# An expert block on one core: where the held scatter of a light quad runs, and the order of the output stage

## The chip, the cores and the metric

One core of a Trainium2 chip runs the whole program. The metric is the device time of one execution in microseconds. The kernel before takes 493.15 us, the median of three runs.

## The reference, cut to what matters

```python
D_MODEL, SEQ, N_GROUPS, EXPERTS_PER_GROUP, TOP_K_INNER, D_EXPERT = 1024, 512, 4, 8, 2, 256

def hierarchical_moe(t, w_group, b_group, w_inner, b_inner, w_gate, w_up, w_down):
    group_p = softmax(t @ w_group + b_group)
    g_w, g_idx = lax.top_k(group_p, 1)
    inner_all = einsum('nd,gde->nge', t, w_inner) + b_inner
    inner_p = softmax(inner_all of the chosen group)
    e_w, e_idx = lax.top_k(inner_p, TOP_K_INNER)
    e_w = e_w / sum(e_w)
    combine = g_w * one_hot(g_idx) * (e_w at e_idx)
    y = zeros_like(t)
    for g in range(N_GROUPS):
        hg = silu(einsum('nd,edf->nef', t, w_gate[g])) * einsum('nd,edf->nef', t, w_up[g])
        y = y + einsum('nef,efd->nd', hg * combine[:, g, :, None], w_down[g])
    return y

def reference(x, ...):
    h = rmsnorm(x, mix_norm)
    x = x + concat([forgetting_attention(h ...), rg_lru(h ...) * gelu(...)]) @ w_out
    x = x + hierarchical_moe(rmsnorm(x, ffn_norm), ...)
    return rmsnorm(x, final_norm)
```

There are 512 tokens in four tiles of 128 and 32 experts. Each expert has three matrices of 1024 x 256 (gate, up) and 256 x 1024 (down) in float32, 3 MB together.

## The kernel before, in words

The attention, the recurrent group, the output projection and the router take about the first half of the span. The change lies in the second half, the experts.

**Quads.** The 32 experts are worked on in eight quads of four. An expert takes at most 32 tokens of each half of the sequence (CAP = 32); a quad's four experts stand side by side on the four groups of 32 partitions. Quads 0 to 5 (groups 0 to 2) are heavy: each treats the two halves of the tokens (hf 0 and 1) one after the other. Quads 6 and 7 (group 3) are light: the experts with few tokens have been sorted there, and one pass of 32 places serves both halves. Quad 6 is the `if light:` branch of the loop over `quads[:-1]`, quad 7 the code behind the loop.

**One pass** consists of these steps:
- `gate_up` multiplies the gathered tokens `xg` with gate and up weights, k = 0 to 7, into one PSUM tile `pg` (tag "mm").
- `places` makes two things out of the 0/1 matrices `s16`: the *front* matmuls against `ident16` transpose them into a PSUM tile `pt` (tag "lg"), and ScalarE copies that to `sT` (the matrix with which results are scattered back to tokens); the *weight* matmuls against `c16` fetch each place's combine weight into `pc`. DVE's `cj`, `cs` and `cw` reduce `pc` to one number for each place. For one half (`len(hfs) == 1`, heavy) `pc` is columns 256 on of the same tile `pt`; for both halves at once (light) `pc` is a tile of its own (tag "tr", printed as ps_pv).
- `hidden` makes `hg`: a tanh on ScalarE, and two operations on DVE, the second of which needs `cw`. `hidden_T` transposes it on TensorE, DVE copies it to `hgT`.
- `down` multiplies with the down weights and splits the result into a high and a low part `y` (ScalarE, then DVE). `scatter` multiplies `sT` with both parts into two PSUM tiles and DVE adds them to `xs`, the running sum (one token tile and one half `n` of the 1024 columns for each add).

**Held scatter.** The last scatters of a quad aren't run at its end. They go into `held` and are run by the next quad, behind its gate-up step k = 0: `held.pop()()`. For a heavy quad these are the scatters of y10 and y11 (second half), for quad 6 those of y1 (both halves).

**Order.** TensorE's instructions and the weight loads keep their program order in this part (`pinned[0] = 1`). DVE's and ScalarE's are ordered by the scheduler of the framework, which tracks what each tile is written and read by and sets the waits. From quad 7's `hidden` on (`pinned[0] = 2`) DVE and ScalarE keep the program order too.

**Loads.** Gate, up and down weights come in 512 KB transfers on SP's queue, in program order, into 18 buffers of 1 MB (`slot` 12, `slot_m` 4, `slot_b` 2); `load_next` issues the next quad's sixteen gate-up loads and eight down loads. A load waits for its buffer's last reader and for room in the queue.

**Output stage.** Behind quad 7's down products: `scatter_to` fills pa and pc (token tiles 0 and 1, columns 0 to 511 and 512 to 1023), pb and pd (token tiles 2 and 3). For pd the running sum has been put into PSUM ahead, by two products with the identity (`mm(pd[t], ident, xs[:, 2 + t, h1], True, False)`), which stand between `hidden_T` and the down products. `square_out` sums squares on ScalarE (and multiplies columns 0 to 511 by `gfin` on POOL), `rsqrt_parts` makes the reciprocal root of a half's sums (ScalarE's square root, small operations on DVE), `write_out` scales (DVE for columns 512 on, with `gfin`; ScalarE for the others) and issues the output's transfer.

Of the kernel before, what the change touches and what calls it, by code (L numbers as in the profile page):

```python
# [53 lines left out]
def block_kernel(ctx, tc, x, mix_norm, w_in, b_forget, conv_w, conv_b, w_a, b_a, w_x, b_x, lru_lambda,  # L54
# [13 lines left out]
    def mm(out_, lhsT, rhs, start, stop):  # L68
        pin(nc.tensor.matmul(out=out_, lhsT=lhsT, rhs=rhs, start=start, stop=stop))  # L69
# [23 lines left out]
    def act(out_, in_, func, **kw):  # L93
        pin(nc.scalar.activation(out=out_, in_=in_, func=func, **kw), 2)  # L94
# [729 lines left out]
    def pst(tag):  # L824
        return psum({"gu": "mm", "gz": "lg", "y": "tr", "tr": "pv"}[tag])
# [159 lines left out]
    def gate_up(pg, xt, gu, q, ks):  # L985
        for k in ks:
            for e in range(4):
                mm(pg[e * CAP:(e + 1) * CAP, :], xt[:, k, q * 4 + e, :],
                   gu[k][e], k == 0, k == KT - 1)

    def places(g, q, hfs, s16):

        n = NS * 3 if g else 12
        pt = pst("gz")
        pc = pst("tr")[:, 0:n] if len(hfs) > 1 else pt[:, 2 * P:2 * P + n]
        sq = [(2 * h + t, s16[h][:, t, q * 4:q * 4 + 4, :].rearrange("p e c -> p (e c)")) for h in hfs for t in range(2)]
        rows = [slice(e * CAP, (e + 1) * CAP) for e in range(4)]
        for i, (t, v) in enumerate(sq):
            for r in rows:
                mm(pt[r, i * P:(i + 1) * P], v[:, r], ident16, True, True)  # L1000
        for i, (t, v) in enumerate(sq):
            c = c16[:, t, 1:].rearrange("p g i e -> p (g i e)") if g else c16[:, t, 0, :, q * 4:q * 4 + 4]
            for r in rows:
                mm(pc[r], v[:, r], c, i == 0, i == len(sq) - 1)
        sT = {}
        for i, h in enumerate(hfs):
            sT[h] = ring_b[0].tile([P, 2, P], F32R, name=f"sT{h}", bufs=1)
            act(sT[h], pt[:, 2 * i * P:2 * (i + 1) * P].rearrange("p (t s) -> p t s", t=2), AF.Copy)
        cw = moe[0].tile([P, 1], F32, name=f"cw{hfs[0]}")
        if g:  # L1010
            sh = [P, NG - 1, 3, EG]
# [9 lines left out]
        else:  # L1021
            cj = moe[0].tile([P, 3, 4], F32, name="cj", bufs=1)
            tt(cj, pc.rearrange("p (i e) -> p i e", i=3), bdm, ALU.mult)
            nc.vector.reduce_sum(out=cw, in_=cj, axis=AX.XY)
        return sT, cw

    def hidden(pg, cw):

# [133 lines left out]
    for i, (g, q) in enumerate(quads[:-1]):  # L1162
# [9 lines left out]
            dns[i + 1] = load_down(ex)  # L1172

        if light:
            gu_k(0, [0])
            held.pop()()
            gu_k(0, range(1, 5))
            sT, cw = places(g, q, (0, 1), sx[g, 0][0])
            gu_k(0, range(5, KT))
            hgT = hidden_T(hidden(pgs[0], cw))  # L1180
            load_next()
            y0 = down(hgT, dns[i], 0)
            y1 = down(hgT, dns[i], 1)
            for hf in range(2):
                scatter(y0, sT[hf], hf, 0)

            def rest(y=y1, sT=sT):
                for hf in range(2):
                    scatter(y, sT[hf], hf, 1)

            held.append(rest)
            continue
        st_ = [sx[g, hf][0] for hf in range(2)]
        if i:
            for k in range(4):
                for hf in range(2):
                    gu_k(hf, [k])
                if k == 0:
                    held.pop()()
            if i == 1:  # L1200
                run(srt)
                ovf = small.tile([P, 1], F32, name="ovf", bufs=1)
# [29 lines left out]
        y10 = split_y(py10)  # L1232
        y11 = down(hgT1, dns[i], 1)

        def rest(y10=y10, y11=y11, sT=sT1[1]):
            scatter(y10, sT, 1, 0)
            scatter(y11, sT, 1, 1)

        held.append(rest)

# [3 lines left out]
    pg = pst("gu")  # L1244
    for k in range(KT):
        gate_up(pg, sx[g, 0][1], gus[i], q, [k])
        if k == 0:
            held.pop()()
        if k == 2:
            sT, cw = places(g, q, (0, 1), sx[g, 0][0])  # L1250
    gfin = ring_b[0].tile([P, D], F32, name="gfin", tag="xg1", bufs=1)
    nc.sync.dma_start(out=gfin, in_=final_norm.partition_broadcast(P))
    yo = [slot()[:, 0:D] for _ in range(NT)]
# [2 lines left out]
    pinned[0] = 2  # L1256
    hg = hidden(pg, cw)
    act(warm, eps, AF.Sqrt)
    hgT = hidden_T(hg, psum("tr"))

    pd = [psum("lg") for _ in range(2)]
    for t in range(2):
        mm(pd[t], ident, xs[:, 2 + t, h1], True, False)
    py = [psum("mm") for _ in range(2)]
    for j in range(2):
        for n in range(2):
            down_mm(py[n], hgT, dns[i], n, [j])
    ys = [split_y(p_) for p_ in py]
    pa, pc, pb = ([psum(a), psum(b)] for a, b in (("lg", "pv"), ("tr", "tr"), ("mm", "mm")))
    scatter_to(pa, ys[0], sT[0])  # L1270
    scatter_to(pc, ys[1], sT[0])
    scatter_to(pb, ys[0], sT[1])
    scatter_to(pd, ys[1], sT[1], False)
    n0, n1 = (rsqrt_parts(hf) for hf in range(2))
    for n, pz in enumerate((pa, pc)):
        for t in range(2):
            scatter_add(pz[t], t, n)
            square_out(t, n, xs[:, t, n * 512:(n + 1) * 512])
    for t in range(2):
        scatter_add(pb[t], 2 + t, 0)  # L1280
    i0 = next(n0)
    for t in range(2):
        square_out(2 + t, 0, xs[:, 2 + t, h0])
    run(n0)
    write_out(0, 1, i0, xs[:, 0, h1])
    for t in range(2):
        square_out(2 + t, 1, pd[t])
    for t in range(2):
        if t:
            write_out(1, 1, i0, xs[:, 1, h1])  # L1290
        write_out(t, 0, i0, None)
    i1 = next(n1)
    run(n1)
    for t in range(2):
        write_out(2 + t, 1, i1, pd[t])
        write_out(2 + t, 0, i1, None)
    for t in range(2):
        act(xs[:, 2 + t, h1], pd[t], AF.Copy)
    pinned[0] = 0


# [85 lines left out]
```

## Time and profile before

| | |
|---|---|
| runs | 492.7, 493.15, 494.58 us; median 493.15 |
| profiled execution | 492.6 us, of it 490.9 us span from the first to the last instruction |
| TensorE busy, weight load | 460.2 us (94% of the span), 285.0 us (58%) |
| DVE, ScalarE, POOL busy | 294.5 us (60%), 192.2 us (39%), 43.5 us (9%) |
| chain that ended last | TensorE 83%, DVE 8%, ScalarE 4% |
| weights moved | 121.20 MB over all queues, mean 247 GB/s |
| quad 6, quad 7 gate-up begin | 436.26 us, 454.52 us |

The page gives busy times and shares of the span; the timeline gives starts in us from the span's first instruction, durations, and in brackets the idle time of the engine ahead of an instruction with what ended it. Merged instructions of one kind carry their count as x8.

### The profile page before, as it was taken

How to read it: one execution, taken by the hardware profiler on the slowest of the kernel's cores; microseconds unless marked ns; L12 is line 12 of the kernel's file. 1: busy time of each engine (PE TensorE's matmuls, PEld its weight loads, DVE VectorE, ACT ScalarE, POOL GpSimd, SP SyncE). 2: the span in 40 equal slices, each digit the busy share in tenths (PEclk: the TensorE clock that was granted, in tenths of full speed). 3: DMA queues.
4: the chain of work that ended last, by engine and by line, in shares of the span. 5: the costliest groups of instructions: out<-in, count | busy, mean ns of one | idle time of the engine just before them, and what ended most of it. 6: DMA issues, size and time to landing. Idle time of an engine off the chain costs nothing.

```text
span 490.9 us, 9409 instructions
## 1 busy us (share of the span) xinstructions
PE 460.2 (94%) x3521; PEld 285.0 (58%) x3521; DVE 294.5 (60%) x761; ACT 192.2 (39%) x407; POOL 43.5 (9%) x89
## 2 busy tenths in 40 slices
PE   6999999989999999999999999999999999998880
PEld 4998677767887787678834345333354343633330
DVE  4959653386899477896675735346363363363554
ACT  6544346735785175655433123111131111211234
POOL 3400001050121021220000000000000000000022
PEclk9999999999999999999999999999999999999995
DMA  8596233204219230050999999999999999999914
GB/s 305 85 251 175 82 89 83 87 0 132 85 48 321 75 115 1 0 171 20 396 383 379 406 364 388 415 408 408 385 414 408 407 414 389 403 400 352 405 55 173
DMA packets 59730, 121.20 MB, mean 247 GB/s; under 512 B 10881, under 2 KB 29345, under 8 KB 59682
## 3 DMA queue, kind: packets, MB, share of 16 engines
q1 hardware_dynamic: 59680, 120.56, 67.9%
q8 instruction: 29, 0.48, 0.4%
q14 instruction: 19, 0.16, 0.1%
q10 hardware_dynamic: 2, 0.00, 0.0%
HBM read 118.45 MB, written 2.10 MB: 246 GB/s over the span
## 4 chain that ended last, share of the span: by engine, by line
PE 83%; DVE 8%; ACT 4%; issue 1%; DMA 1%; POOL 0%; SPq 0%; ACTq 0%; DVEq 0%; POOLq 0%
PE ps_mm L69 48%; PE ps_lg L69 18%; PE ps_tr L69 10%; PE ps_pv L69 4%; PE ps_tr L79 3%; DMA slot<-in_w_in_dram 1%; DVE hold L393 1%; DVE hg L88 1%; ACT slot L94 1%; DVE h2l L88 1%; ACT hold L94 1%; DVE xs L82 1%; DVE s L82 1%; ACT hg L94 1%; DVE slot L82 0%
## 5 line engine op out<-in xcount | busy, mean ns | idle before, releaser
L69 PE MATMUL ps_mm<-slot 128*128 128x512 f32 (+1 forms) x576 | 120.7, 366 | 3.1 <-DVE kS L82 2.8
L69 PEld LDWEIGHTS ps_mm<-slot 128*128 128x128 f32 x576 | 96.3, 192 | 22.9 <-issue 5.1
L69 PE MATMUL ps_mm<-slot,xg 128*32 128x512 f32 x688 | 102.2, 594 | 0.0
L69 PEld LDWEIGHTS ps_mm<-slot,xg 128*32 128x32 f32 x688 | 25.6, 110 | 38.0 <-issue 36.2
L82 DVE TENSOR_TENSOR xs<-xs,ps_lg 128x512 f32<-128x512 f32 x57 | 35.5, 682 | 12.2 <-PE ps_lg L69 12.0
L82 DVE TENSOR_TENSOR slot<-slot 128x1024 fp32r<-128x1024 f32 (+1 forms) x27 | 32.9, 1221 | 13.4 <-ACT slot L94 13.4
L94 ACT ACTIVATE hg<-ps_mm 128x256 f32<-128x256 f32 x14 | 5.4, 384 | 82.4 <-PE ps_mm L69 80.3
L94 ACT ACTIVATE y<-ps_tr 128x512 fp32r<-128x512 f32 x26 | 15.5, 597 | 48.1 <-PE ps_tr L69 36.4
L69 PE MATMUL ps_lg<-y,sT 128*128 128x512 f32 x118 | 33.5, 421 | 0.1
L94 ACT ACTIVATE slot<-slot 128x1024 fp32r<-128x1024 f32 (+1 forms) x28 | 29.2, 1055 | 7.6 <-DMA slot<-in_w_in_dram 5.9
L88 DVE SCALAR_TENSOR_TENSOR hg<-hg,ps_mm 128x256 f32<-128x256 f32 x14 | 5.9, 420 | 43.6 <-ACT hg L94 43.6
L69 PEld LDWEIGHTS ps_lg<-y,sT 128*128 128x128 f32 x118 | 19.9, 187 | 19.7 <-issue 10.1
L69 PE MATMUL ps_lg<-s,hold 128*128 128x256 f32 x128 | 30.5, 323 | 0.6 <-ACT s L94 0.6
L82 DVE TENSOR_TENSOR y<-ps_tr,y 128x512 fp32r<-128x512 f32 x26 | 17.9, 687 | 20.3 <-ACT y L94 20.3
L558 POOL TENSOR_TENSOR ql<-qT,qh 64x128 fp32r<-64x128 f32 x32 | 19.6, 614 | 110.5 <-ACT qh L94 96.3
L1084 POOL TENSOR_TENSOR slot<-xs,gfin 128x512 f32<-128x512 f32 x4 | 5.5, 1392 | 264.4 <-ACT slot L94 264.4
L69 PE MATMUL ps_mm<-slot_m,xg 128*32 128x512 f32 x128 | 28.8, 593 | 0.0
L69 PE MATMUL ps_lg<-s,h2l 128*128 128x256 f16 x128 | 27.0, 278 | 1.5 <-DVE h2l L88 0.9
L69 PE MATMUL ps_mm<-slot,hold 128*128 128x512 f32 x96 | 26.0, 408 | 0.0
L69 PE MATMUL ps_mm<-slot,oT 128*128 128x512 f32 x96 | 24.6, 401 | 0.5 <-DVE oT L82 0.5
L94 ACT ACTIVATE pe<-ps_lg,nb 128x128 f32<-128x128 f32 (+3 forms) x32 | 16.8, 526 | 18.3 <-DVE nb L85 13.1
L69 PE MATMUL ps_tr<-slot,hgT 128*32 128x512 f32 x192 | 23.4, 595 | 0.0
(256 smaller groups left out, 724.3 us busy)
## 6 DMA issues: line engine op xcount, KB each, us to landing
slot<-in_w_gate_dram SPq DMA_DIRECT2D x42, 512.0 KB, 10.2
slot<-in_w_up_dram SPq DMA_DIRECT2D x42, 512.0 KB, 10.2
slot<-in_w_down_dram SPq DMA_DIRECT2D x32, 512.0 KB, 10.8
slot_m<-in_w_down_dram SPq DMA_DIRECT2D x24, 512.0 KB, 10.1
slot<-in_w_in_dram SPq DMA_DIRECT2D x16, 512.0 KB, 3.8
slot<-in_w_out_dram SPq DMA_DIRECT2D x8, 512.0 KB, 4.1
slot<-in_w_gate_dram SPq DMA_DIRECT2D x16, 256.0 KB, 6.1
slot<-in_w_up_dram SPq DMA_DIRECT2D x16, 256.0 KB, 5.3
```

The costliest lines, as they stand in the source:

```text
L69: pin(nc.tensor.matmul(out=out_, lhsT=lhsT, rhs=rhs, start=start, stop=stop))
L79: pin(nc.tensor.transpose(out=out_, in_=in_, identity=ident[0:n, 0:n]))
L82: return pin(nc.vector.tensor_tensor(out=out_, in0=a, in1=b, op=op), 2)
L88: pin(nc.vector.scalar_tensor_tensor(out=out_, in0=a, scalar=s, in1=b, op0=op0, op1=op1), 2)
L94: pin(nc.scalar.activation(out=out_, in_=in_, func=func, **kw), 2)
L393: nc.vector.tensor_tensor_scan(out=ti_[:, c, :], data0=tr_[:, c, :], data1=xc[:, c, :], initial=0.0, op0=ALU.mult, op1=ALU.add)
L558: nc.gpsimd.tensor_tensor(out=ql[own, hh], in0=src, in1=qh[own, hh].bitcast(F32), op=ALU.subtract)
L1084: nc.gpsimd.tensor_tensor(out=yo[t][:, sl], in0=src, in1=gfin[:, sl], op=ALU.mult)
```

## The change

`places` is split into `places_front` (front matmuls and the copies to `sT`) and `place_weights` (weight matmuls and `cw`). `places`, which the heavy quads still call, runs the one and then the other; the copies thereby stand ahead of the weight matmuls in the program. The light quads call the two separately: `place_weights` behind gate-up step k = 4, `places_front` behind `hidden_T`. The held scatter of the quad before takes an argument, which of its two parts to run; in a light quad its part 0 stands between `hidden` and `hidden_T`, its part 1 behind `hidden_T`. Heavy quads run both parts where they did.

In the output stage the running sum that is put into PSUM ahead is that of token tiles 0 and 1 (pc) and no longer that of 2 and 3 (pd), and the two identity products stand between the first and the second halves of the down products. The order of adds, squares, roots and writes follows the token order that this gives.

```diff
                 mm(pg[e * CAP:(e + 1) * CAP, :], xt[:, k, q * 4 + e, :],
                    gu[k][e], k == 0, k == KT - 1)
 
+    rows = [slice(e * CAP, (e + 1) * CAP) for e in range(4)]
+
     def places(g, q, hfs, s16):
 
-        n = NS * 3 if g else 12
         pt = pst("gz")
-        pc = pst("tr")[:, 0:n] if len(hfs) > 1 else pt[:, 2 * P:2 * P + n]
-        sq = [(2 * h + t, s16[h][:, t, q * 4:q * 4 + 4, :].rearrange("p e c -> p (e c)")) for h in hfs for t in range(2)]
-        rows = [slice(e * CAP, (e + 1) * CAP) for e in range(4)]
-        for i, (t, v) in enumerate(sq):
+        return places_front(q, hfs, s16, pt), place_weights(g, q, hfs, s16, pt)
+
+    def quad_places(q, hfs, s16):
+        return [(2 * h + t, s16[h][:, t, q * 4:q * 4 + 4, :].rearrange("p e c -> p (e c)")) for h in hfs for t in range(2)]
+
+    def places_front(q, hfs, s16, pt=None):
+        pt = pst("gz") if pt is None else pt
+        for i, (t, v) in enumerate(quad_places(q, hfs, s16)):
             for r in rows:
                 mm(pt[r, i * P:(i + 1) * P], v[:, r], ident16, True, True)
+        sT = {}
+        for i, h in enumerate(hfs):
+            sT[h] = ring_b[0].tile([P, 2, P], F32R, name=f"sT{h}", bufs=1)
+            act(sT[h], pt[:, 2 * i * P:2 * (i + 1) * P].rearrange("p (t s) -> p t s", t=2), AF.Copy)
+        return sT
+
+    def place_weights(g, q, hfs, s16, pt=None):
+        n = NS * 3 if g else 12
+        pc = pst("tr")[:, 0:n] if pt is None else pt[:, 2 * P:2 * P + n]
+        sq = quad_places(q, hfs, s16)
         for i, (t, v) in enumerate(sq):
             c = c16[:, t, 1:].rearrange("p g i e -> p (g i e)") if g else c16[:, t, 0, :, q * 4:q * 4 + 4]
             for r in rows:
                 mm(pc[r], v[:, r], c, i == 0, i == len(sq) - 1)
-        sT = {}
-        for i, h in enumerate(hfs):
-            sT[h] = ring_b[0].tile([P, 2, P], F32R, name=f"sT{h}", bufs=1)
-            act(sT[h], pt[:, 2 * i * P:2 * (i + 1) * P].rearrange("p (t s) -> p t s", t=2), AF.Copy)
         cw = moe[0].tile([P, 1], F32, name=f"cw{hfs[0]}")
         if g:
             sh = [P, NG - 1, 3, EG]
@@ -1022,7 +1033,7 @@
             cj = moe[0].tile([P, 3, 4], F32, name="cj", bufs=1)
             tt(cj, pc.rearrange("p (i e) -> p i e", i=3), bdm, ALU.mult)
             nc.vector.reduce_sum(out=cw, in_=cj, axis=AX.XY)
-        return sT, cw
+        return cw
 
     def hidden(pg, cw):
 
@@ -1172,20 +1183,23 @@
             dns[i + 1] = load_down(ex)
 
         if light:
-            gu_k(0, [0])
-            held.pop()()
-            gu_k(0, range(1, 5))
-            sT, cw = places(g, q, (0, 1), sx[g, 0][0])
+            gu_k(0, range(5))
+            cw = place_weights(g, q, (0, 1), sx[g, 0][0])
             gu_k(0, range(5, KT))
-            hgT = hidden_T(hidden(pgs[0], cw))
+            hg = hidden(pgs[0], cw)
+            rest = held.pop()
+            rest([0])
+            hgT = hidden_T(hg)
+            rest([1])
+            sT = places_front(q, (0, 1), sx[g, 0][0])
             load_next()
             y0 = down(hgT, dns[i], 0)
             y1 = down(hgT, dns[i], 1)
             for hf in range(2):
                 scatter(y0, sT[hf], hf, 0)
 
-            def rest(y=y1, sT=sT):
-                for hf in range(2):
+            def rest(parts, y=y1, sT=sT):
+                for hf in parts:
                     scatter(y, sT[hf], hf, 1)
 
             held.append(rest)
@@ -1196,7 +1210,7 @@
                 for hf in range(2):
                     gu_k(hf, [k])
                 if k == 0:
-                    held.pop()()
+                    held.pop()(range(2))
             if i == 1:
                 run(srt)
                 ovf = small.tile([P, 1], F32, name="ovf", bufs=1)
@@ -1232,9 +1246,9 @@
         y10 = split_y(py10)
         y11 = down(hgT1, dns[i], 1)
 
-        def rest(y10=y10, y11=y11, sT=sT1[1]):
-            scatter(y10, sT, 1, 0)
-            scatter(y11, sT, 1, 1)
+        def rest(parts, y10=y10, y11=y11, sT=sT1[1]):
+            for n in parts:
+                scatter((y10, y11)[n], sT, 1, n)
 
         held.append(rest)
 
@@ -1244,10 +1258,8 @@
     pg = pst("gu")
     for k in range(KT):
         gate_up(pg, sx[g, 0][1], gus[i], q, [k])
-        if k == 0:
-            held.pop()()
-        if k == 2:
-            sT, cw = places(g, q, (0, 1), sx[g, 0][0])
+        if k == 4:
+            cw = place_weights(g, q, (0, 1), sx[g, 0][0])
     gfin = ring_b[0].tile([P, D], F32, name="gfin", tag="xg1", bufs=1)
     nc.sync.dma_start(out=gfin, in_=final_norm.partition_broadcast(P))
     yo = [slot()[:, 0:D] for _ in range(NT)]
@@ -1256,46 +1268,53 @@
     pinned[0] = 2
     hg = hidden(pg, cw)
     act(warm, eps, AF.Sqrt)
+    rest = held.pop()
+    rest([0])
     hgT = hidden_T(hg, psum("tr"))
-
-    pd = [psum("lg") for _ in range(2)]
+    rest([1])
+    sT = places_front(q, (0, 1), sx[g, 0][0])
+    py = [psum("mm") for _ in range(2)]
+    for n in range(2):
+        down_mm(py[n], hgT, dns[i], n, [0])
+
+    pc = [psum("lg") for _ in range(2)]
     for t in range(2):
-        mm(pd[t], ident, xs[:, 2 + t, h1], True, False)
-    py = [psum("mm") for _ in range(2)]
-    for j in range(2):
-        for n in range(2):
-            down_mm(py[n], hgT, dns[i], n, [j])
+        mm(pc[t], ident, xs[:, t, h1], True, False)
+    for n in range(2):
+        down_mm(py[n], hgT, dns[i], n, [1])
     ys = [split_y(p_) for p_ in py]
-    pa, pc, pb = ([psum(a), psum(b)] for a, b in (("lg", "pv"), ("tr", "tr"), ("mm", "mm")))
+    pa, pb, pd = ([psum(a), psum(b)] for a, b in (("lg", "pv"), ("tr", "tr"), ("mm", "mm")))
     scatter_to(pa, ys[0], sT[0])
-    scatter_to(pc, ys[1], sT[0])
+    scatter_to(pc, ys[1], sT[0], False)
     scatter_to(pb, ys[0], sT[1])
-    scatter_to(pd, ys[1], sT[1], False)
+    scatter_to(pd, ys[1], sT[1])
     n0, n1 = (rsqrt_parts(hf) for hf in range(2))
-    for n, pz in enumerate((pa, pc)):
-        for t in range(2):
-            scatter_add(pz[t], t, n)
-            square_out(t, n, xs[:, t, n * 512:(n + 1) * 512])
+    for t in range(2):
+        scatter_add(pa[t], t, 0)
+        square_out(t, 0, xs[:, t, h0])
     for t in range(2):
         scatter_add(pb[t], 2 + t, 0)
+        square_out(t, 1, pc[t])
+    scatter_add(pd[0], 2, 1)
     i0 = next(n0)
     for t in range(2):
         square_out(2 + t, 0, xs[:, 2 + t, h0])
     run(n0)
-    write_out(0, 1, i0, xs[:, 0, h1])
     for t in range(2):
-        square_out(2 + t, 1, pd[t])
+        write_out(t, 1, i0, pc[t])
+        if t == 0:
+            scatter_add(pd[1], 3, 1)
     for t in range(2):
-        if t:
-            write_out(1, 1, i0, xs[:, 1, h1])
+        square_out(2 + t, 1, xs[:, 2 + t, h1])
+    i1 = next(n1)
+    for t in range(2):
         write_out(t, 0, i0, None)
-    i1 = next(n1)
     run(n1)
     for t in range(2):
-        write_out(2 + t, 1, i1, pd[t])
+        write_out(2 + t, 1, i1, xs[:, 2 + t, h1])
         write_out(2 + t, 0, i1, None)
     for t in range(2):
-        act(xs[:, 2 + t, h1], pd[t], AF.Copy)
+        act(xs[:, t, h1], pc[t], AF.Copy)
     pinned[0] = 0
```

## Rows read from the trace of the kernel before

**Rows 1.** The page, part 1 (busy us, share of the span, instructions of each engine) and part 4 (shares of the chain that ended last).

```profile
PE 460.2 (94%) x3521; PEld 285.0 (58%) x3521; DVE 294.5 (60%) x761; ACT 192.2 (39%) x407; POOL 43.5 (9%) x89
...
PE 83%; DVE 8%; ACT 4%; issue 1%; DMA 1%; POOL 0%; SPq 0%; ACTq 0%; DVEq 0%; POOLq 0%
```

**Rows 2.** Busy time by windows: one stretch of 20 us in the expert part. Columns: stretch, sum, TensorE, weight load, DVE, ScalarE, POOL (instructions), granted clock, share of the DMA engines, GB/s.

```profile
360.00:380.00 20.00, 20.00 (x176) 9.64 (x172) 9.34 (x15) 4.07 (x8) 0.00 (x0) 1.00 1.03 410
```

**Rows 3.** Timeline of quad 2 (heavy), both calls of places: start, duration, engine, line. The weight matmuls are ps_lg<-c,s, the copy is sT, hg is the tanh; the last row is hidden_T of the second half.

```profile
322.36 0.25 PE L69 MATMUL ps_lg<-c,s 128*32 128x72 f16 x8
...
322.50 0.38 ACT L94 ACTIVATE hg<-ps_mm 128x256 f32<-128x256 f32 x1 [11.99 <-PE ps_mm L69]
...
322.78 0.38 ACT L94 ACTIVATE sT<-ps_lg 128x256 fp32r<-128x256 f32 x1
...
326.44 0.25 PE L69 MATMUL ps_lg<-c,s 128*32 128x72 f16 x8
...
326.94 0.38 ACT L94 ACTIVATE sT<-ps_lg 128x256 fp32r<-128x256 f32 x1
...
329.26 0.65 PE L69 MATMUL ps_pv<-ident,hg 128*32 128x128 f32 x16 [0.85 <-DVE hg L88]
```

**Rows 4.** Timeline of quad 0, first call of places.

```profile
261.46 0.21 PE L69 MATMUL ps_lg<-c,s 128*32 128x12 f16 x8
...
262.18 0.38 ACT L94 ACTIVATE sT<-ps_lg 128x256 fp32r<-128x256 f32 x1
...
262.66 0.17 DVE L82 TENSOR_TENSOR cj<-ps_lg,bdm 128x12 f32<-128x12 f32 x1 [0.53 <-ACT sT L94]
```

**Rows 5.** Three views: all of ScalarE's copies sT of the heavy quads (tile view, 261 to 421 us: durations in ns least/median/most, first and last start); what TensorE waited for in 261 to 430 us (us in total, times, longest); and the timeline of quad 5's second half, a gather matmul.

```profile
L94 ACT ACTIVATE sT<-ps_lg x12: 378/378/382, 262.2 to 417.4; 128x256 fp32r<-128x256 f32 x12
...
PE ps_pv L69 <- DVE hg L88: 2.5, 4, 0.9
...
419.60 0.39 PE L69 MATMUL ps_lg<-s,hold 128*128 128x256 f32 x1 [0.40 <-ACT s L94]
```

**Rows 6.** Timeline of quad 6 (light): copies sT, cj, the tanh of hg, hidden_T, the down products.

```profile
443.31 0.66 ACT L94 ACTIVATE sT<-ps_lg 128x256 fp32r<-128x256 f32 x2 [6.17 <-PE ps_lg L69]
...
443.47 0.54 DVE L88 SCALAR_TENSOR_TENSOR cj<-rank,slotid,ps_pv 128x24 f32<-128x24 f32 x3 [2.99 <-PE ps_pv L69]
...
446.09 0.38 ACT L94 ACTIVATE hg<-ps_mm 128x256 f32<-128x256 f32 x1 [2.12 <-PE ps_mm L69]
...
447.59 0.65 PE L69 MATMUL ps_pv<-ident,hg 128*32 128x128 f32 x16 [1.62 <-DVE hg L88]
...
448.77 3.64 PE L69 MATMUL ps_tr<-slot_m,hgT 128*32 128x512 f32 x32 [0.54 <-DVE hgT L91]
```

**Rows 7.** Timeline of quad 7 and the output stage's start: the held scatter, the front matmuls, gate-up step 4 of the first experts, the tanh of hg, hidden_T, the identity products, the down products, the first result's copy y.

```profile
455.51 2.24 PE L69 MATMUL ps_lg<-y,sT 128*128 128x512 f32 x8
...
459.43 0.41 PE L69 MATMUL ps_lg<-ident,s 128*32 128x128 f16 x16
...
460.64 0.60 PE L69 MATMUL ps_mm<-slot_b,xg 128*32 128x512 f32 x2
...
464.32 0.38 ACT L94 ACTIVATE hg<-ps_mm 128x256 f32<-128x256 f32 x1 [3.73 <-PE ps_mm L69]
...
465.82 0.64 PE L69 MATMUL ps_tr<-ident,hg 128*32 128x128 f32 x16 [1.57 <-DVE hg L88]
...
466.40 1.98 PE L69 MATMUL ps_lg<-xs,ident 128*128 128x512 f32 x4
...
468.31 4.07 PE L69 MATMUL ps_mm<-slot,hgT 128*32 128x512 f32 x32
...
471.56 0.60 ACT L94 ACTIVATE y<-ps_mm 128x512 fp32r<-128x512 f32 x1 [5.34 <-PE ps_mm L69]
```

**Rows 8.** The weight stream at its end: SP's issues of loads (start, duration with the gaps of merged ones), what SP waited for in 426 to 437 us and in 451 to 462 us (us in total, times, longest), and the weight load of TensorE that waited for the last down load.

```profile
435.61 0.33 SPq L104 DMA_DIRECT2D slot<-in_w_gate_dram  x1
...
448.32 0.33 SPq L104 DMA_DIRECT2D slot<-in_w_up_dram  x1
...
450.47 9.78 SPq L104 DMA_DIRECT2D slot<-in_w_down_dram  x8
...
SPq L104 <- PE ps_tr L69: 1.7, 1, 1.7
...
SPq L104 <- DMA slot<-in_w_up_dram: 1.3, 2, 0.7
...
470.48 0.14 PEld L69 LDWEIGHTS ps_mm<-slot,hgT 128*32 128x32 f32 x5 [0.30 <-DMA slot<-in_w_down_dram]
```

**Rows 9.** Timeline of the output stage: two adds from PSUM, POOL's second pair of products, DVE's products with gfin (first from xs, then from PSUM), the second square root, ScalarE's last two scalings.

```profile
474.85 1.28 DVE L82 TENSOR_TENSOR xs<-xs,ps_tr 128x512 f32<-128x512 f32 x2
...
478.80 2.94 POOL L1084 TENSOR_TENSOR slot<-xs,gfin 128x512 f32<-128x512 f32 x2 [1.04 <-ACT slot L94]
...
479.05 3.24 DVE L88 SCALAR_TENSOR_TENSOR slot<-xs,fin,gfin 128x512 f32<-128x512 f32 x2 [0.15 <-DVE fin L88]
...
482.39 0.29 ACT L94 ACTIVATE fin<-fin,eps 128x2 f32<-128x2 f32 x1 [0.69 <-DVE fin L82]
...
483.51 1.41 DVE L88 SCALAR_TENSOR_TENSOR slot<-ps_lg,fin,gfin 128x512 f32<-128x512 f32 x2
...
483.56 1.33 ACT L94 ACTIVATE slot<-slot,fin 128x512 f32<-128x512 f32 x2 [0.88 <-DVE fin L88]
```

## The prediction

> **What bounds the kernel now.** I read the page first, for the shares of the engines and of the chain: TensorE is busy in 94% of the span and carries 83% of the chain that ended last, so a TensorE second saved or lost anywhere in the expert part normally counts [rows 1]. Then the windows of the expert part, for the rival bound: TensorE is filled there, but the DMA engines are as well, at some 400 GB/s [rows 2]. There are two bounds side by side, the matmuls and the weight stream, and which one ends last is to be asked stage by stage. So I went on with the timeline around every place where the diff touches the order of TensorE: the placing matmuls of the six heavy quads [rows 3 to 5], the two light quads [rows 6, 7], the last loads [rows 8], and the output stage [rows 9].
>
> **Part 1, the split of places: heavy quads.** The diff speaks of light quads, but `places` is called twelve times by the six heavy ones, and there it changes the program order. Before: the eight front matmuls (into columns 0 to 255 of one PSUM tile), the eight weight matmuls (into columns 256 on of the same tile), then ScalarE's copy sT. After: front, copy, weight matmuls. The columns differ, so no value passes from the copy to the weight matmuls; the question is whether the order of two engines on one PSUM bank is kept all the same.
>
> The trace has a case. In quad 0, DVE's cj reads the weight columns and ScalarE's sT reads the front columns. The weight matmuls began at 261.46 and were done by 261.7, DVE was idle, and yet cj began at 262.66, right behind the end of sT (262.18 + 0.38), with 0.53 us of idle time put down to sT [rows 4]. In the light quad, where the two lie in different banks, sT (443.31 to 443.97 for both) and cj (443.47) run side by side [rows 6]. So accesses to one bank by different engines are kept in program order, whatever the columns. This row is of two readers; a matmul that writes behind a reader is not in the trace.
> The Trainium skill, "PSUM — Partial Sum Buffer", section "PSUM bank collisions raise a hardware error", states it for all pairs: two engines on the same bank and partitions at once collide even on disjoint columns, and the compiler's scheduler puts a dependency between any two of them, reads and writes alike. By that rule the weight matmuls wait for the copy and the sum is the one below; by the row of the two readers alone it could also be that of the first rival.
>
> I take it that the weight matmuls wait. Price, from quad 2 [rows 3]: first half, weight matmuls at 322.36, the copy ends at 322.78 + 0.38 = 323.16 (it stands behind the tanh of 322.50, which was ready earlier); second half 326.44 against 327.32. That is 0.80 and 0.88; with a handover between 0 and the 0.10 of [rows 4], 0.05 taken, 0.85 and 0.93. TensorE runs in program order, so everything behind stands still: the other half's gate-up products, or the down products. Twelve calls (all twelve copies take 0.378 us [rows 5]): 6 x 0.85 + 6 x 0.93 = 10.7, and 0.3 more in quad 0's first, where the copy came late behind xg (262.56 against 261.46). Together 11.0.
> What hides some: TensorE already waits four times for DVE's hg, 2.5 us in all [rows 5]. Two of these (0.85 each, as at 329.26) follow so closely that hg itself slips by about a quarter us, the length of the weight matmuls; so 2.0 of the 2.5 cover. In quad 5's second half the gather waits until 419.60 for ScalarE's s anyway [rows 5], which covers one stall of 0.93. Heavy quads: 11.0 - 2.0 - 0.9 = **+8.0 us**. Bounds: 5.5 (the copy scheduled ahead of the tanh, 0.3 less a call, a little of it paid back through hg) to 9.5 (0.1 a call for refilling TensorE).
>
> **Part 2, quad 6.** Out of the gate-up products go the held scatter (2.24 us of TensorE, as its twin at 455.51 [rows 7]) and the front matmuls (half of the 0.4 from 459.43 on, 0.2). Today TensorE stands from the end of gate-up at 446.0 to 447.59 for hg, and from 448.24 to 448.77 for hgT [rows 6]. The first half of the scatter (1.1) fits into the first gap. Behind hidden_T come the other half (1.1) and the front (0.3): 1.4 where 0.5 was idle, so down starts 0.9 later relative to the end of gate-up. Net -2.24 - 0.2 + 0.9 = **-1.5**. The scatter's four adds on DVE stand beside hg's two operations; if the scheduler puts one between them, hg comes 0.64 later, so -0.9 is the other end.
>
> **Part 3, quad 7.** Gate-up is shorter by the same **-2.4**. Then, from its end (464.25): hidden_T as now from +1.57 to +2.2 [rows 7]; scatter half and front to +3.65 (DVE's copy of hgT waits behind two adds, till +3.1, covered); first down halves 1.75; the identity products of x, 1.95 [rows 7], which today fill the hgT gap and now stand in the open; one down half 1.05: the first result at +8.4, where it is +7.3 now (464.25 to 471.56). **+1.1**, bounds 0.8 and 1.8.
>
> **The weight stream.** SP's waits there are for landings, so an issue marks the landing of the load eight earlier. The last gate-up load (448.32) thus landed shortly before the last of the eight down loads was issued, 450.47 + 9.78 - 0.33 = 459.92, and the last down load is what a TensorE weight load waited for at 470.48 [rows 8]. Today quad 7 uses the fourth expert's second half from 460.6 on: 0.6 us of slack. If TensorE came 3.9 us earlier (parts 2 and 3 without part 1) it would wait for that load. With part 1 it comes 8.0 - 1.5 - 2.2 = 4.3 later, and the stream, whose issue at 435.61 waits for quad 5's down products, moves by 8: twelve loads from there to the last gate-up one, 1.35 us each [rows 8], end near 443.6 + 2 + 15 = 460 to 461, against a use at about 465. Not the bound; cost nothing.
>
> **Part 4, the output.** For t = 0, 1 the sum stays in PSUM. Today the two products with gfin, both operands in SBUF, take 1.62 us each while POOL works (479.05, POOL 478.80 to 481.74); the same from PSUM takes 0.70 (483.51, 1.41 for two) [rows 9]. After: product 0.70, an add 0.64, product 0.70 = 2.05 against 3.24, -1.2 on DVE; five adds before the first reciprocal instead of six, but they wait for TensorE's later scatters, so its start stays. ScalarE gets less: its first two scalings move behind the second square root (482.39), and four then stand in a row, 4 x 0.67 [rows 9], ending only 0.2 earlier. The eight output issues follow. I take **-0.6**, bounds 0 and -1.4.
>
> **Sum.** 8.0 - 1.5 - 2.4 + 1.1 - 0.6 = **+4.6 us**. The profiled execution took 492.6 (span 490.9 and 1.7 around it); that gives 497.2. The median of the three runs lies 0.55 higher: **497.7**. With all terms at one end +1.0 and +8.7; two or three off together give +2.2 to +6.7, that is 495.3 to 499.8 for this case alone.
>
> **Rivals.**
> *No order on the bank between copy and matmul.* Part 1 falls to nothing. Then the loads decide: quad 7 resumes when the last gate-up load lands, about 460.05 instead of 460.65, -0.4 after the weight matmuls moved there; +1.1 behind it and -0.6 at the output: +0.1, 493.2. For it: different columns, no data. Against: the 0.53 of quad 0.
> *Faster: no order, and the loads not a floor.* Place: quad 7's fifth gate-up step. If the last gate-up load lands before 457 and the last down load before 468, all of -1.5 - 2.4 + 1.1 - 0.6 = -3.4 comes through, 489.7. It decides only where the loads come 2.5 us earlier than now; nothing in the diff moves their issue.
> *The wait is there but mostly hidden*, the copies early, more of it under hg's chain: Part 1 about 5, the sum +0.9 to +2.4, 494 to 495.5. Against: after ten of the twelve calls no wait long enough follows.
>
> **How the numbers follow.** A measurement of this kernel tells about 0.5%, 2.5 us, from no change. Bank order holds 0.82, of it 0.09 so well hidden that it stays under 2.5 us; no order and loads the floor 0.11 (0.10 within 0.5%, 0.01 faster); faster 0.05; 0.02 for what I don't see, half to either side. Slower 0.74, same 0.19, faster 0.07. The range 493.0 to 500.3 holds the first case but for its ends and takes in the hidden one and part of the first rival.
>
> **What would show it.** In the profile after, the weight matmuls of each heavy quad start behind the end of sT and not right behind the front, with idle time on TensorE put down to ACT sT, some 0.85 each; quads 1 to 4 last 1 to 2 us longer; quad 6's gate-up starts near 444; TensorE's gap behind its last gate-up product holds four scatters; DVE's first two gfin products take 0.7. The forecast is wrong if the weight matmuls still start right behind the front, or if quad 7 stands waiting for a load.

## The result: 1.0% slower, as forecast

The changed kernel takes 498.19 us (median of four runs, 497.06 to 500.47) where the kernel before takes 493.03 beside it: +5.2 us, a ratio of 1.0104 with a 95% interval of 1.0063 to 1.0146. The forecast was 497.7. The profiled execution, the shortest of the four, took 497.06 us, with a span of 495.4 against 490.9.

The page of the changed kernel, parts 1 and 4 [rows 1 before]:

```profile
PE 461.3 (93%) x3521; PEld 286.8 (58%) x3521; DVE 293.4 (59%) x761; ACT 192.2 (39%) x407; POOL 44.7 (9%) x89
...
PE 84%; DVE 6%; ACT 6%; issue 1%; DMA 1%; POOL 0%; ACTq 0%; DVEq 0%; POOLq 0%
```

The number of instructions is the same on every compute engine. TensorE's busy time is 1.1 us more, in a span that is 4.5 us longer, and its share of the span falls by one point: most of the added time is idle time. Where it sits is said by the view of waits of the changed kernel, 240 to 478 us (engine, tile and line that waited, for what: us in total, times, longest), two of its lines:

```profile
PE ps_lg L69 <- ACT sT L94: 8.7, 12, 1.0
...
PE ps_pv L69 <- DVE hg L88: 1.0, 1, 1.0
```

The first line did not exist before: twelve waits, one for each call of places in the heavy quads. The second had four waits in the heavy quads [rows 5] and has none there now; the one that is left is quad 6's. In quad 2 (timeline; front matmuls, copy sT, weight matmuls, for both halves, then hidden_T) it looks like this where [rows 3] show before:

```profile
325.27 0.29 PE L69 MATMUL ps_lg<-ident,s 128*32 128x128 f16 x8
...
325.80 0.38 ACT L94 ACTIVATE sT<-ps_lg 128x256 fp32r<-128x256 f32 x1
...
326.23 0.25 PE L69 MATMUL ps_lg<-c,s 128*32 128x72 f16 x8 [0.67 <-ACT sT L94]
...
330.17 0.30 PE L69 MATMUL ps_lg<-ident,s 128*32 128x128 f16 x8
...
330.77 0.38 ACT L94 ACTIVATE sT<-ps_lg 128x256 fp32r<-128x256 f32 x1
...
331.20 0.25 PE L69 MATMUL ps_lg<-c,s 128*32 128x72 f16 x8 [0.74 <-ACT sT L94]
...
333.43 0.64 PE L69 MATMUL ps_pv<-ident,hg 128*32 128x128 f32 x16 [0.17 <-PE ps_tr L69]
```

The copy ends at 325.80 + 0.38 = 326.18 and the weight matmuls begin 0.05 later, 0.96 behind the front's beginning. In the kernel before they began 0.11 behind it (322.36 in [rows 3], and this line):

```profile
322.25 0.29 PE L69 MATMUL ps_lg<-ident,s 128*32 128x128 f16 x8
```

In quad 0, where the copy comes late (261.50), the wait is the longest:

```profile
261.50 0.38 ACT L94 ACTIVATE sT<-ps_lg 128x256 fp32r<-128x256 f32 x1
...
261.93 0.22 PE L69 MATMUL ps_lg<-c,s 128*32 128x12 f16 x8 [0.97 <-ACT sT L94]
```

Quad 6's gate-up begins at 443.47 and not at 436.26. The two light quads then win some of it back, and the output stage some more; the terms are gone through below, step by step.

### The profile page after: what moved, and what is told of

Same layout as the page of the kernel before. It is cut to its first block, busy times and chain, and to the rows that moved or that the text cites. A ratio compares the mean times of both kernels' runs of the same rounds, so it can differ in the third digit from the quotient of the medians.

```text
span 495.4 us, 9422 instructions
## 1 busy us (share of the span) xinstructions
PE 461.3 (93%) x3521; PEld 286.8 (58%) x3521; DVE 293.4 (59%) x761; ACT 192.2 (39%) x407; POOL 44.7 (9%) x89
## 4 chain that ended last, share of the span: by engine, by line
PE 84%; DVE 6%; ACT 6%; issue 1%; DMA 1%; POOL 0%; ACTq 0%; DVEq 0%; POOLq 0%
PE ps_mm L69 49%; PE ps_lg L69 18%; PE ps_tr L69 11%; PE ps_pv L69 4%; PE ps_tr L79 3%; DVE hold L393 1%; ACT hg L94 1%; DVE h2l L88 1%; ACT slot L94 1%; ACT hold L94 1%; ACT sT L94 1%; DMA xs<-in_x_dram 1%; DVE xs L82 1%; DVE slot L82 0%; ACT h L94 0%
```

## The experiments

The theory: the heavy quads' weight matmuls wait for the copy because both touch one PSUM bank, this costs about 8 us by quad 6, and what the light quads and the output stage gain (some 3.4 us) would be cut off by the weight stream if the heavy quads didn't lose first. The rivals: the loss sits in the light quads or the output stage; the order of the program alone makes the wait; the stream is no floor.

**heavy_old.** The changed kernel with the old order for the heavy quads alone (`places` as before, copies behind the weight matmuls):

```diff
     def places(g, q, hfs, s16):
-        pt = pst("gz")
-        return places_front(q, hfs, s16, pt), place_weights(g, q, hfs, s16, pt)
+        ...   # the body of the kernel before
```

> The changed kernel, but the six heavy quads keep the order of before in places (copies behind the weight matmuls); light quads and output stage as changed. Theory of the prediction (the twelve waits of the weight matmuls for sT are the whole loss): no such wait, quad 6 starts near 436.3 us as before, then quad 7 stands for the last gate-up load, which lands near 459.9; time 492.5 to 493.7, within 0.5% of before. Rival that the loads are no floor: the gain of the light quads and of the output stage comes through whole, 489 to 490. Rival that the loss sits in the light quads or the output stage: 496 to 498.

Measured: 493.02 us, ratio to the kernel before 1.0009 (95% interval 0.999 to 1.0027). The whole loss is gone with the order of two steps in the heavy quads, and nothing is won: quad 7 waits for its last gate-up load. Timeline and windows (stretch, sum, TensorE, weight load, DVE, ScalarE, POOL, granted clock, DMA share, GB/s):

```profile
461.10 1.03 PE L69 MATMUL ps_mm<-slot,xg 128*32 128x512 f32 x1 [1.61 <-DMA slot<-in_w_up_dram]
...
458.00:460.00 2.00, 1.04 (x2) 0.14 (x2) 0.00 (x0) 0.00 (x0) 0.00 (x0) 1.00 1.03 416
460.00:462.00 2.00, 0.90 (x14) 0.30 (x15) 0.00 (x0) 0.00 (x0) 0.00 (x0) 0.70 1.02 404
462.00:464.00 2.00, 2.00 (x17) 0.81 (x19) 0.70 (x4) 0.00 (x0) 0.00 (x0) 0.50 1.03 414
```

The granted clock was not expected: it fell to half, 1.2 of 2.4 GHz, behind this wait, and the matmuls of step 4 and 5 took 1.03 us and not 0.60. The twelve executions of this kernel fall into two groups, 491.0 to 493.3 (seven) and 494.8 to 495.8 (five); the profiled one, 495.29, is of the second.

**own_bank.** The changed kernel, copies still first in the program, weight matmuls in a bank of their own:

```diff
-        return places_front(q, hfs, s16, pt), place_weights(g, q, hfs, s16, pt)
+        return places_front(q, hfs, s16, pt), place_weights(g, q, hfs, s16)
```

> The changed kernel, but the heavy quads' weight matmuls write a PSUM tile of their own (the one that the light quads use for it) instead of columns of the tile that the copy reads; the copies stay ahead of them in the program. Theory that the order is kept because both touch one bank: no wait for sT, the same time as with the old order, 492.5 to 493.7. Rival that the order of the program alone makes the wait, whatever the bank: twelve waits of some 0.7 us, 497 to 499 as changed.

Measured: 493.77, ratio 1.0025 (1.0009 to 1.0041); no matmul waits for sT any more. Quad 2's first half:

```profile
321.57 0.25 PE L69 MATMUL ps_pv<-c,s 128*32 128x72 f16 x8
...
321.99 0.38 ACT L94 ACTIVATE sT<-ps_lg 128x256 fp32r<-128x256 f32 x1
...
459.72 0.59 PE L69 MATMUL ps_mm<-slot,xg 128*32 128x512 f32 x1 [1.59 <-DMA slot<-in_w_up_dram]
```

The weight matmuls (now ps_pv) run 0.4 us ahead of the copy that precedes them in the program. So the program order alone does not make the wait; sharing tile and bank with the copy does. The edit gives the weight matmuls another tile as well as another bank, and no run puts two tiles into one bank, so it is not shown which of the two the framework's scheduler goes by. The last line is quad 7's wait for the load again. The median is 0.1 above the window expected, still far from 497.

**split_only.** The kernel before with the copies moved ahead of the weight matmuls, and nothing else:

```diff
+        sT = {}
+        for i, h in enumerate(hfs):
+            ...
         for i, (t, v) in enumerate(sq):
             c = ...
             for r in rows:
                 mm(pc[r], v[:, r], c, i == 0, i == len(sq) - 1)
-        sT = {}
-        for i, h in enumerate(hfs):
-            ...
```

> The kernel before, with one edit: in places the copies stand ahead of the weight matmuls. Theory: twelve waits for sT, 8.7 us of idle time in all, quad 6 starts some 7.2 us later; the held scatter and the output stage as before, and quad 7's 0.4 us for the last down load goes away: plus 6.5 to 7, 499.5 to 500.2. Rival that the waits are hidden by the weight stream and the loss of the change lies elsewhere: under 495.

Measured: 501.86, ratio 1.0184 (1.0168 to 1.02): +9, more than expected. The view of waits has the same line, 8.7 us in twelve, and quad 6 starts at 444.24. The profiled execution took 500.16, +7.5 on the span: the 7.9 that the heavy quads lose, less the 0.4 us for the last down load. The other three, which have no profile, took 501.75 to 502.35.

**split_again.** The same kernel and the same diff, once more.

> The same as split_only, for a second profile: that one's profiled execution (500.16 us) was 1.7 us under the other three. Theory that the twelve waits are the same in every execution: quad 6 starts 7.9 us later against the first gather as in the first profile; what the slower executions add, if one is caught, lies in front of the experts or in quad 7's wait for loads.

Measured: 501.72 and 502.04, the latter profiled. The twelve waits are again 8.7 us. What the slower execution adds is in neither of the two places that I had named, but in quad 6: its down products, first the profile of split_only, then that of split_again with two windows of 1 us:

```profile
456.76 3.64 PE L69 MATMUL ps_tr<-slot_m,hgT 128*32 128x512 f32 x32 [0.54 <-DVE hgT L91]
```

```profile
456.97 5.29 PE L69 MATMUL ps_tr<-slot_m,hgT 128*32 128x512 f32 x32 [0.54 <-DVE hgT L91]
...
455.00:456.00 1.00, 0.21 (x8) 0.24 (x12) 0.61 (x2) 0.00 (x0) 0.00 (x0) 1.00 0.74 238
456.00:457.00 1.00, 0.46 (x20) 0.20 (x13) 0.42 (x1) 0.00 (x0) 0.00 (x0) 0.97 0.98 258
457.00:458.00 1.00, 1.00 (x8) 0.34 (x12) 0.00 (x0) 0.00 (x0) 0.00 (x0) 0.50 0.95 279
```

Behind the two gaps around hidden_T the granted clock fell to half and the down products took 1.65 us more. That is all but 0.2 us of the difference of the two profiled executions (1.88 in device time). The three executions of split_only without a profile lie where this one does; that the clock fell in them as well is not shown. In the changed kernel, where scatters fill these gaps, the clock stayed at 1.00 through quad 6, and so it did in the profile of before.

**output_only.** The kernel before with the new output stage alone:

```diff
-    pd = [psum("lg") for _ in range(2)]
+    pc = [psum("lg") for _ in range(2)]
     for t in range(2):
-        mm(pd[t], ident, xs[:, 2 + t, h1], True, False)
+        mm(pc[t], ident, xs[:, t, h1], True, False)
     ...   # down products as before, output stage as changed
```

> The kernel before, with the output stage of the changed one alone (x of token tiles 0 and 1 put into PSUM, other token order); the two identity products stay ahead of the down products, so nothing ahead of the output moves. Theory: minus 0.6 us (0 to minus 1.4), 491.7 to 493.0; DVE's first two products 0.75 us each instead of 1.62. Rival that the late add of the last token tile costs more than it saves: plus 0.3 to 1.

Measured: 492.11, ratio 0.9985 (0.9976 to 0.9994): -0.7 us by the ratio, -0.5 between the medians. This is the size expected, a small gain whose interval excludes no change.

**quad6_only.** The kernel before with quad 6 alone as changed (its held scatter as two parts, `place_weights` behind step 4, `places_front` behind hidden_T).

```diff
+            cw = place_weights(g, q, (0, 1), sx[g, 0][0])   # behind step 4
...
+            rest = held.pop()
+            rest([0])
+            hgT = hidden_T(hg)
+            rest([1])
+            sT = places_front(q, (0, 1), sx[g, 0][0])
```

> The kernel before with quad 6 alone changed (held scatter in the two gaps around hidden_T, front behind it); heavy quads, quad 7 and the output stage as before. Theory: quad 7 starts 1.3 us earlier, but its step 4 had only 0.6 us of slack at its last gate-up load and the last down load ends at the same time: 492.2 to 493.2, no change that can be measured. Rival that the gain comes through: 491.0 to 491.5.

Measured: 492.45, ratio 0.9991 (0.9979 to 1.0004). No change can be told from this, as the theory has it; in the profile quad 7's matmul waits 0.9 us for its last gate-up load.

**fewer_loads.** heavy_old, with quad 7's weight stream cut:

```diff
-            gus[i + 1] = load_gate_up(ex, 4)
+            gus[i + 1] = load_gate_up(ex, 4, 4 if i + 1 == len(quads) - 1 else KT)   # gu[k] = gu[k - 4] for the rest
```

> The kernel of heavy_old, but quad 7's eight gate-up loads for k = 4 to 7 are left out, and its steps 4 to 7 multiply with the weights of steps 0 to 3 (part of quad 7's weights is thus not used). TensorE's instructions are the same. Theory that the weight stream is the floor of the light quads' gain: quad 7 no longer waits, the gain of the light quads and of the output stage comes through, minus 3 to minus 4 us against before, 488.5 to 490. Rival that the wait in quad 7 is something else, or that the time behind it would grow by what is saved: 492 to 493.5.

Measured: 489.69, ratio 0.9938 (0.9923 to 0.9953). The first down result's copy starts at 468.72, 2.8 us ahead of before [rows 7]:

```profile
468.72 0.60 ACT L94 ACTIVATE y<-ps_mm 128x512 fp32r<-128x512 f32 x1 [4.00 <-PE ps_mm L69]
```

**before_fewer_loads.** The control, the kernel before with the same loads left out.

```diff
-            gus[i + 1] = load_gate_up(ex, 4)
+            gus[i + 1] = load_gate_up(ex, 4, 4 if i + 1 == len(quads) - 1 else KT)
```

> The control: the kernel before with the same eight loads of quad 7 left out (its steps 4 to 7 use the weights of steps 0 to 3). Theory: before had 0.6 us of slack at these loads and waited 0.3 to 0.4 for the last down load, so only that comes off: 492.0 to 492.6. Rival that before was bound by the stream as well: under 491.

Measured: 492.54, ratio 0.999 (0.9978 to 1.0002). Between the two kernels without these loads the light quads and the output stage are worth 2.9 us; with them (heavy_old against before), nothing that can be told.

**fill_load_wait.** heavy_old, with the filling work where quad 7 waits for its load:

```diff
-        if k == 4:
+        if k == 0:
+            held.pop()(range(2))
+        if k == 2:
+            sT = places_front(q, (0, 1), sx[g, 0][0])
             cw = place_weights(g, q, (0, 1), sx[g, 0][0])
+        if k == 3:
+            ...   # the identity products into pc
...   # these are left out behind hidden and hidden_T
```

> The kernel of heavy_old, but in quad 7 the held scatter goes back behind step 0, both halves of places behind step 2 and the identity products behind step 3, so that they fill the time in which quad 7 waits for its last gate-up load, and nothing but the down products stands behind hidden_T. Theory: the first down result waits for the last down load only, minus 0.3 there and minus 0.5 in the output stage: 491.5 to 492.3, faster than both kernels. Rival that the load wait shows up later with the same end as heavy_old: 492.5 to 493.5.

Measured: 492.48, ratio 0.9985 (0.997 to 1.0001), between the two windows expected (491.5 to 492.3, rival 492.5 to 493.5), so neither is borne out. In the profiled execution (493.0 us) the gap behind gate-up is empty again, the clock fell behind it, and the down products took 5.34 us (4.07 in [rows 7]). Whether that happened in the other executions is not shown.

```profile
468.02 5.34 PE L69 MATMUL ps_mm<-slot,hgT 128*32 128x512 f32 x32 [0.54 <-DVE hgT L91]
...
466.00:468.00 2.00, 0.65 (x16) 0.41 (x16) 1.08 (x3) 1.22 (x2) 0.00 (x0) 1.00 0.75 305
468.00:470.00 2.00, 1.98 (x12) 0.59 (x16) 0.00 (x0) 0.00 (x0) 0.00 (x0) 0.59 0.29 111
```

**busy_wait.** heavy_old, with four unused identity products behind step 3 that keep TensorE at work:

```diff
+        if k == 3:
+            idle = pst("gz")
+            for t in range(4):
+                mm(idle, ident, xs[:, t, h0], True, True)
```

> The kernel of heavy_old with four products of the identity with x behind quad 7's step 3, into a PSUM tile that nothing reads: some 3.9 us of work for TensorE while it would wait for its last gate-up loads anyway. Theory: the wait itself costs what it did, but the granted clock, which fell to half for about 4 us behind that wait in the profile of heavy_old, stays at full; the executions near 495 us of heavy_old (five of twelve) vanish, median 491.5 to 492.7. Rival that these executions come from the loads: the same two groups of times, median about 493.

Measured: 493.13 (492.15 to 494.46), ratio 0.9995 (0.9978 to 1.0011). The profile has the clock at 1.00 in every window from 452 to 472 us, and no execution lies between 494.8 and 495.8, where five of heavy_old's did. That fits the clock as the cause of the upper group, with one profile of each kernel. But the median did not come down to 491.5 to 492.7; it is the "about 493" of the rival. Whether the products delay step 4 where the load came early was not tried, and this half stays open.

**q6_and_output.** The kernel before with quad 6 and the output stage changed, heavy quads and quad 7 as before:

```diff
+            rest([0])
+            hgT = hidden_T(hg)
+            rest([1])
...
-        mm(pd[t], ident, xs[:, 2 + t, h1], True, False)
+        mm(pc[t], ident, xs[:, t, h1], True, False)
```

> The kernel before with quad 6 changed and the changed output stage; heavy quads and quad 7 up to its down products as before (identity products for token tiles 0 and 1). Theory: quad 6's gain ends at quad 7's loads, the output stage gives its 0.5 to 0.7 us: 492.0 to 492.7 where before takes 492.6 to 493.0, a ratio of 0.997 to 0.999, faster than both kernels. Rival that quad 6's gain adds to it: ratio under 0.996.

Measured: 492.01, ratio 0.9977 (0.9964 to 0.999): faster than both kernels, as expected. The output stage alone gave 0.9985; whether quad 6 adds anything to it the intervals do not tell.

## Why the prediction was right, step by step

Measured in the two profiled executions, with the chain's first matmul group of the expert part as the start. Before, then changed:

```profile
233.19 5.63 PE ps_mm L69 x24
```

```profile
232.52 5.63 PE ps_mm L69 x24
```

The changed execution came 0.7 us earlier to the experts, with the same instructions up to there: jitter, which the sum below leaves out.

*Part 1, +8.0 forecast.* From there to quad 6's gate-up: 443.47 - 232.52 = 210.95 against 436.26 - 233.19 = 203.07, **+7.9**. The step that carried the prediction was the one row of [rows 4], two readers of one bank kept in order; the changed kernel's waits show it for a matmul behind a reader as well, and own_bank that they go where the two share neither tile nor bank. The rule of the Trainium skill, "PSUM — Partial Sum Buffer", section "PSUM bank collisions raise a hardware error", is that a dependency is put between any two engines on a bank, reads and writes alike. The twelve waits of 8.7 us agree with it. The price of a call was right: in quad 2 the weight matmuls stand 0.96 and 1.03 behind the front and not 0.11, that is 0.85 and 0.92 later, and the twelve calls together come to 10.9, where 11.0 was forecast. (The waits of 8.7 are less, because they count from the front's end.)

The cover was right by luck. 10.9 - 7.9 = 3.0 us were hidden and 2.9 forecast, but the parts differ. At the four waits for hg 0.6 was hidden each time, 2.4 in all and not 2.0. Quad 5's gather hid 0.5 and not 0.9: the line of [rows 5] has 0.40 us of idle time, and DVE's s, which the gather waits for, now comes later as well, behind cj.

*Part 2, -1.5.* Quad 6 takes 460.39 - 443.47 = 16.92 instead of 18.26: **-1.3**. The bound that I had named came true in part: the scheduler put one add of the scatter between hg's two operations, at 451.53. From the tanh to hidden_T it now takes 1.98 us and not 1.50 [rows 6].

```profile
443.47 4.47 PE L69 MATMUL ps_mm<-slot,xg 128*32 128x512 f32 x40
...
450.58 1.19 PE L69 MATMUL ps_lg<-y,sT 128*128 128x512 f32 x4
...
450.77 0.38 ACT L94 ACTIVATE hg<-ps_mm 128x256 f32<-128x256 f32 x1 [6.43 <-PE ps_mm L69]
...
451.53 0.68 DVE L82 TENSOR_TENSOR xs<-xs,ps_lg 128x512 f32<-128x512 f32 x1
...
452.75 0.64 PE L69 MATMUL ps_pv<-ident,hg 128*32 128x128 f32 x16 [0.97 <-DVE hg L88]
...
454.68 3.61 PE L69 MATMUL ps_tr<-slot_m,hgT 128*32 128x512 f32 x32
```

*Part 3, -2.4 and +1.1.* Gate-up of quad 7 from 460.39 to 468.2 is 7.8 us instead of 9.73: **-1.9**. From its end to the first result's copy 8.5 instead of 7.3: **+1.15**, by the order forecast:

```profile
468.17 1.20 PE L69 MATMUL ps_lg<-y,sT 128*128 128x512 f32 x4
...
469.78 0.64 PE L69 MATMUL ps_tr<-ident,hg 128*32 128x128 f32 x16 [0.42 <-DVE hg L88]
...
473.54 1.98 PE L69 MATMUL ps_lg<-xs,ident 128*128 128x512 f32 x4
...
476.66 0.60 ACT L94 ACTIVATE y<-ps_mm 128x512 fp32r<-128x512 f32 x1 [4.00 <-PE ps_mm L69]
```

*The weight stream, nothing forecast: here a step failed.* I had the last gate-up load land at 460 to 461, 4 us ahead of its use. By the same reading (the issue eight loads later marks the landing) it landed shortly before 455.16 + 9.57 - 0.33 = 464.40, just as TensorE came to it, and step 4 lost the 0.5 us that are missing from -2.4. (The profile names no load there; it has 0.51 us without a weight load at 464.49. The load as its cause is inferred from the landing.) By the prediction's last sentence a quad 7 that waits for a load is a sign of a wrong forecast: in this step it was one. SP's issues and that weight load, SP's wait for quad 5's down products (us, times, longest), and the windows behind:

```profile
442.83 0.33 SPq L104 DMA_DIRECT2D slot<-in_w_gate_dram  x1
...
452.82 0.33 SPq L104 DMA_DIRECT2D slot<-in_w_up_dram  x1
...
455.16 9.57 SPq L104 DMA_DIRECT2D slot<-in_w_down_dram  x8
...
464.49 0.14 PEld L69 LDWEIGHTS ps_mm<-slot,xg 128*32 128x32 f32 x2 [0.51 <-issue]
```

```profile
SPq L104 <- PE ps_tr L69: 5.6, 1, 5.6
```

```profile
443.00:445.00 2.00, 2.00 (x24) 0.65 (x20) 1.03 (x2) 0.60 (x1) 0.00 (x0) 1.00 0.68 236
...
449.00:451.00 2.00, 2.00 (x18) 0.63 (x11) 0.30 (x2) 0.23 (x1) 0.00 (x0) 1.00 1.00 301
...
455.00:457.00 2.00, 2.00 (x24) 0.60 (x20) 0.38 (x1) 0.84 (x3) 0.00 (x0) 1.00 0.88 250
...
459.00:461.00 2.00, 2.00 (x14) 0.96 (x16) 2.00 (x4) 0.00 (x0) 0.00 (x0) 1.00 1.02 418
```

The restart at 442.83 was forecast within 0.8 us; the twelve loads behind it were counted at the pace of the last eight, 1.35 us each, but the stream gives 236 to 336 GB/s in the windows from 443 to 457 and not 410, and the landing came 21.6 us behind the restart where 17 were counted. A stretch like that was there before as well (246 to 332 GB/s in 445 to 451), and I had not put it into the sum. In 443 to 445 the DMA engines are only 0.68 busy, behind SP's wait; where the rest of it comes from, with the engines near full, no run shows. So the stream lay at the edge of becoming the bound even in the slower kernel.

*Part 4, -0.6.* From the first result's copy to the end of the span 18.74 instead of 19.34: **-0.6**. DVE's two products take 0.75 and 0.74 beside POOL, against 1.62 in [rows 9], and ScalarE's four scalings stand in a row, as the price said:

```profile
483.81 2.50 POOL L1095 TENSOR_TENSOR slot<-xs,gfin 128x512 f32<-128x512 f32 x2 [1.03 <-ACT slot L94]
...
484.06 0.75 DVE L88 SCALAR_TENSOR_TENSOR slot<-ps_lg,fin,gfin 128x512 f32<-128x512 f32 x1
...
486.59 2.54 ACT L94 ACTIVATE slot<-slot,fin 128x512 f32<-128x512 f32 x4
...
487.50 1.42 DVE L88 SCALAR_TENSOR_TENSOR slot<-xs,fin,gfin 128x512 f32<-128x512 f32 x2
```

The last line shows what the prediction's two prices left open: with both operands in SBUF, but with POOL done (486.31), a product takes 0.71. The 1.62 came with POOL at work beside it.

*Sum.* 7.9 - 1.3 - 1.9 + 1.15 - 0.6 = +5.2, where +4.6 was forecast; the 0.6 are the load wait, the add in quad 6, and rounding. The medians differ by 5.2 too, but that agreement is partly chance: the two profiled executions differ by 4.5, and the sum leaves out the 0.7 by which the changed one was ahead at the experts. In the forecast's own range the upper end was added up wrongly: 9.5 - 0.9 - 2.4 + 1.8 - 0 is +8.0 and not +8.7.

*The rivals.* "No order on the bank" was the kernel own_bank: its price, +0.1 us against before by the load floor, was right in kind (+1.2 measured, 0.4 to 2.0 by the interval; heavy_old +0.4, within its interval of nothing). The difference is not settled; the halved clock behind the load wait, which heavy_old shows, is one candidate and was not seen in own_bank's one profile. "Loads not a floor" was priced at -3.4 and came to -3.1 with the loads taken away; the condition, loads some 2.5 us earlier, is not met by anything in the change. "Mostly hidden" had part 1 at about 5; it came to 7.9.

## What to carry to other kernels

When a helper is split, ask what its other callers' program order becomes: here the gain was meant for two light quads, and six heavy ones paid for it because two steps use different columns of one tile in one bank. Give results that different engines read or write a bank each, or keep all writes ahead of the first read. Where matmuls and a weight stream are both near full, price a gain of the one against the slack of the other first: the 3 us that the light quads and the output stage save did not show until the loads were cut. And a gap on TensorE can cost more than its own length where the granted clock falls behind it, as in split_again.

## What was not expected of the hardware

The granted clock fell to half behind pairs of gaps on TensorE of 0.5 to 1.6 us, and that in one execution and not in another of the same kernel. Behind quad 6's gaps (TensorE busy 0.17 + 0.21 + 0.46 us in 454 to 457) it fell in split_again, which cost 1.65 us in the down products alone, and stayed at 1.00 in split_only with the same gaps. Behind heavy_old's two load waits (0.94 and 1.61 us; 1.55 us of work in 457 to 461) it was 0.50 until about 464. In the profile of own_bank, with one load wait of 1.59, it stayed at 1.00, and so it did in that of busy_wait, with work in that place.
